# Seven block products for five pairs of w_down's row blocks, in a two-layer decoder on one core

## The chip, the cores and the metric

The kernel runs on one core of a Trainium2 chip. The metric is the device time of one execution in microseconds (us), lower is better. The chip's engines run side by side and wait for each other by semaphores: TensorE (PE; its weight loads are listed apart as PEld), VectorE (DVE), ScalarE (ACT), GpSimd (POOL), and SyncE (SP), which here issues the loads from HBM.

## The reference

Two decoder layers over 256 tokens of width 1024, in float32. Layer 0 has block-sparse attention (with 256 tokens, one causal block) and layer 1 a forgetting attention. What the change touches is the second half of each layer, the MLP with a hidden width of 4096:

```python
def squared_relu_mlp(x, w_up, w_down):
    return jnp.square(jax.nn.relu(x @ w_up)) @ w_down

# in each layer, h being 256 x 1024:
h = h + merge_heads(mix) @ w_o[layer]
h = h + squared_relu_mlp(rms_norm(h, mlp_norm[layer]), w_up[layer], w_down[layer])
# after the last layer
return rms_norm(h, final_norm)
```

w_down is 4096 x 1024 per layer, so the product with it has 256 rows, 4096 terms and 1024 columns.

## The kernel before, in words

Each float32 operand is split into a high part (`hi`, rounded) and the rest (`lo`), and a product is three matmuls: high by high, high by low and low by high. For a weight, `split` (L143) makes both parts: ACT copies a piece of 128 x 1024 values to `hi` (L148), and DVE subtracts to get `lo` (L149).

Weights come in chunks of 1 MB by one DMA each, into three buffers called `raw` (pool `wraw`). There are seven buffers for high parts and seven for low parts (`whi`, `wlo`), each for one piece of 128 x 1024; a chunk fills two. A list `plan` holds the order of all chunks. `chunk(i)` (L191) is called by every step that multiplies; it sees to it that the loads and splits up to two chunks further on have been written into the program. A load waits for its `raw` buffer, that is for the last DVE instruction on the chunk three places earlier. A split waits for the `hi` and `lo` buffers, that is for the last matmul on the piece seven places earlier.

A row block of w_down is 128 of its 4096 rows; there are 32. The hidden activations `hid` are kept transposed, as 32 blocks of 128 x 256 (two halves of 128 tokens), high and low. With `row_chunk` (L153) a chunk of w_down is four row blocks by 512 columns. `mm_rows` (L196) multiplies one half of one hidden block by one row block into a PSUM bank of 128 x 512: three matmuls of 512 columns. The product is run first for columns 0 to 511 (nb=0) over all 32 blocks and both halves, then for columns 512 to 1023 (nb=1): 2 x 32 x 2 x 3 = 384 matmuls per layer. After each nb, `down_done` (L780) adds the two banks to `h`. In layer 0 the norm of the next layer then begins on these columns (`norm_steps`, L279), while TensorE goes on with nb=1.

In layer 1 the code after the loop (L799 to L824) runs nb=1: all blocks but the last eight for both halves in turn, then the last eight for half 0, then for half 1, and after each half the final norm of that half: add to `h` (L778), sum of squares on ACT (L813), mean on DVE (L815), the power -0.5 on POOL (L818), the scaling on ACT and DVE (L820, L823), and two output DMAs.

Before the product with w_down, `put_up` (L713) makes the hidden blocks two at a time from PSUM: ACT copies one part (L723), DVE adds the other (L724), squares (L726), ACT rounds to the high part (L727) and DVE subtracts (L728). This is the up stage; a chunk of w_up holds two hidden blocks.

The order of TensorE is written out by a planner (`Weave`) that takes steps from lists by due times; within w_down the steps stand in the order in which the code makes them. The order of DVE and ACT is chosen by a scheduler when the program is built; each engine then runs its instructions strictly in that order.

PSUM has eight banks, in three pools: `psa` (three, tiles named acc), `pss` (four, sc), `psv` (one, pv). The small work tiles `t` (pool `tmp`) have six buffers.

Of the kernel before, what the change touches and what calls it, by code (L numbers as in the profile page):

```python
# [8 lines left out]
F32 = mybir.dt.float32  # L9
# [5 lines left out]
P = 128  # L15
D = 1024
# [46 lines left out]
def yoco_kernel(  # L63
# [160 lines left out]
    hid = []

# [382 lines left out]
    for layer in range(2):  # L608
# [99 lines left out]


        hid.clear()  # L710


        def put_up(fc, accs):  # L713
# [12 lines left out]
            nc.vector.scalar_tensor_tensor(sq[:, 0:n], u[:, 0:n], 0.0, u[:, 0:n], op0=ALU.max, op1=ALU.mult)  # L726
            nc.scalar.copy(hh[:, a], sq[:, 0:n])  # L727
# [52 lines left out]
        def down_done(nb, ps):  # L780
# [5 lines left out]
            if layer:  # L786

                nc.vector.tensor_scalar(part, sums[:, :, 0], 1.0 / D, EPS, op0=ALU.mult, op1=ALU.add)

        edge = []  # L790
        for nb in range(2 - layer):
            fill += rows_steps(take(FF // NB), hid, lambda ps, nb=nb: down_done(nb, ps),
                               pe.after((("h", nb, 0), 850), (("h", nb, 1), 1500)))
# [5 lines left out]
    cs = take(FF // NB)  # L799
    ps = [psa.tile([P, NB], F32, name="acc") for _ in range(2)]  # L800

    def last_part(half, k):
        mm_rows(ps[half], *hidden(k), half, chunk(cs[k // CK]), k % CK, k == 0, k == FF // P - 1)

    for k in range(FF // P - 2 * CK):
        for half in range(2):
            last_part(half, k)
    for half in range(2):
        for k in range(FF // P - 2 * CK, FF // P):
            last_part(half, k)  # L810
        add_mlp(1, half, ps[half])
# [42 lines left out]
```

## Time and profile before

| | us |
|---|---|
| median of three runs (lowest to highest) | 599.67 (599.61 to 599.84) |
| the profiled execution | 599.86 |
| its span, first to last instruction and DMA | 598.1 |
| TensorE busy in the span | 587.9 |
| VectorE busy | 399.2 |
| ScalarE busy | 325.2 |

The profiled execution is 1.76 us longer than its span. Busy shares are averages over stages. In the trace of before, the up stage of layer 0 lies at about 121 to 210 us, its w_down at 210 to 298 us; those of layer 1 lie at about 414 to 503.5 us and 503.5 to 590.8 us. A matmul's listed length (0.39 us) overlaps with its neighbours'; what it costs in a row of matmuls is the distance from start to start. The granted TensorE clock was 0.998 of full speed over the execution.

### The profile page before, as it was taken

What the parts mean: (1) busy time and instruction counts of PE and PEld (TensorE: products, weight loads), DVE (VectorE), ACT (ScalarE), POOL (GpSimd) and SP (SyncE); (2) the same over time, 40 slices, a digit from 0 to 9 for tenths busy, and PEclk for the clock granted to TensorE, in tenths of its full rate; (3) what the DMA queues carried; (4) which work ended last, traced back from release to release, by engine and by line L of the source; (5) the groups of instructions that cost most, each with busy time, mean ns of one, the idle gap of its engine ahead of it and who ended that gap; (6) DMA issues with size and microseconds to landing.
All of it is one profiled execution on the core that took longest, in us unless ns stands there. A gap on an engine that the chain in (4) does not pass through costs nothing.

```text
span 598.1 us, 8745 instructions
## 1 busy us (share of the span) xinstructions
PE 587.9 (98%) x3412; PEld 506.0 (85%) x3412; DVE 399.2 (67%) x715; ACT 325.2 (54%) x563; POOL 10.1 (2%) x39
## 2 busy tenths in 40 slices
PE   8999999999999999999999999999999999999995
PEld 6998997888888888888889989978888888888884
DVE  5887477488877854564588976668788778446422
ACT  6776566566655644363474664666666555334411
POOL 3000000000000000000000000000000000000000
PEclk9999999999999999999999999999999999999999
DMA  8974443467655655555546444543766656555401
GB/s 269 315 267 141 141 141 88 131 190 227 208 169 187 211 187 171 206 196 182 185 143 210 141 142 141 173 143 94 213 188 208 171 184 212 186 178 199 142 0 72
DMA packets 77034, 103.94 MB, mean 174 GB/s; under 512 B 1800, under 2 KB 51504, under 8 KB 76992
## 3 DMA queue, kind: packets, MB, share of 16 engines
q1 hardware_dynamic: 76480, 102.26, 52.8%
q8 instruction: 27, 0.44, 0.3%
q0 software_dynamic: 208, 0.59, 0.3%
q10 hardware_dynamic: 304, 0.53, 0.2%
q14 instruction: 15, 0.12, 0.1%
HBM read 102.32 MB, written 1.05 MB: 173 GB/s over the span
## 4 chain that ended last, share of the span: by engine, by line
PE 97%; DMA 1%; SPq 0%; DVE 0%; ACT 0%; POOLq 0%; issue 0%
PE acc L216 19%; PE acc L199 14%; PE acc L201 14%; PE acc L200 14%; PE acc L220 9%; PE acc L207 5%; PE acc L209 5%; PE acc L208 5%; PE sc L356 2%; PE pv L368 1%; DMA h<-in_x_dram 1%; PE sc L216 1%; PE sc L324 1%; PE sc L322 1%; PE sc L269 1%; PE sc L220 1%
## 5 line engine op out<-in xcount | busy, mean ns | idle before, releaser
L149 DVE TENSOR_TENSOR lo<-raw,hi 128x1024 fp32r<-128x1024 f32 x188 | 229.0, 1222 | 114.0 <-ACT hi L148 113.0
L148 ACT ACTIVATE hi<-raw 128x1024 fp32r<-128x1024 f32 x188 | 198.4, 1061 | 133.8 <-PE acc L201 99.4
L216 PE MATMUL acc<-x,hi 128*128 128x512 f32 x480 | 164.6, 396 | 0.0
L199 PE MATMUL acc<-hi,b 128*128 128x512 f32 x320 | 126.3, 395 | 0.0
L201 PE MATMUL acc<-hi,b 128*128 128x512 f32 x320 | 124.8, 390 | 0.0
L200 PE MATMUL acc<-lo,b 128*128 128x512 f32 x320 | 124.6, 390 | 0.0
L220 PE MATMUL acc<-x,lo 128*128 128x256 f32 x480 | 124.3, 279 | 0.0
L216 PEld LDWEIGHTS acc<-x,hi 128*128 128x128 f32 x480 | 86.1, 188 | 16.2
L220 PEld LDWEIGHTS acc<-x,lo 128*128 128x128 f32 x480 | 90.5, 189 | 5.3
L207 PE MATMUL acc<-x,hi 128*128 128x256 f32 x256 | 74.1, 289 | 0.0
L209 PE MATMUL acc<-x,lo 128*128 128x256 f32 x256 | 72.4, 283 | 0.0
L208 PE MATMUL acc<-x,hi 128*128 128x256 f32 x256 | 72.4, 283 | 0.0
L199 PEld LDWEIGHTS acc<-hi,b 128*128 128x128 f32 x320 | 60.1, 188 | 12.9 <-issue 1.0
L201 PEld LDWEIGHTS acc<-hi,b 128*128 128x128 f32 x320 | 60.1, 188 | 12.8
L200 PEld LDWEIGHTS acc<-lo,b 128*128 128x128 f32 x320 | 60.2, 188 | 11.9
L723 ACT COPY t<-acc 128x256 f32<-128x256 f32 x60 | 22.4, 373 | 63.6 <-PE acc L216 61.1
L207 PEld LDWEIGHTS acc<-x,hi 128*128 128x128 f32 x256 | 49.0, 191 | 1.8 <-issue 1.7
L208 PEld LDWEIGHTS acc<-x,hi 128*128 128x128 f32 x256 | 49.0, 192 | 0.1
L209 PEld LDWEIGHTS acc<-x,lo 128*128 128x128 f32 x256 | 49.0, 192 | 0.0
L724 DVE TENSOR_TENSOR t<-acc,t 128x256 f32<-128x256 f32 x60 | 25.0, 420 | 20.5 <-ACT t L723 20.4
L341 ACT ACTIVATE t<-t,nm 128x128 f32<-128x128 f32 x64 | 28.3, 443 | 7.6 <-DVE nm L334 7.6
L727 ACT CAST b<-t 128x512 fp32r<-128x512 f32 (+1 forms) x36 | 20.6, 571 | 6.7 <-DVE t L726 6.7
(129 smaller groups left out, 523.6 us busy)
## 6 DMA issues: line engine op xcount, KB each, us to landing
raw<-in_w_up_dram SPq DMA_DIRECT2D x32, 1024.0 KB, 5.5
raw<-in_w_down_dram SPq DMA_DIRECT2D x32, 1024.0 KB, 5.1
raw<-in_moba_w_qkv_dram SPq DMA_DIRECT2D x10, 1024.0 KB, 5.2
raw<-in_w_o_dram SPq DMA_DIRECT2D x8, 1024.0 KB, 4.9
raw<-in_w_kv_dram SPq DMA_DIRECT2D x8, 1024.0 KB, 5.4
raw<-in_fox_w_q_dram SPq DMA_DIRECT2D x4, 1024.0 KB, 4.9
raw<-in_moba_w_qkv_dram SPq DMA_DIRECT2D x3, 512.0 KB, 7.9
h<-in_x_dram SPq DMA_DIRECT2D x2, 256.0 KB
```

The source lines that it names most:

```text
L148: nc.scalar.activation(hi[:, i:i + n], raw[:, i:i + n], AF.Copy)
L149: nc.vector.tensor_sub(lo[:, i:i + n], raw[:, i:i + n], f(hi[:, i:i + n]))
L199: nc.tensor.matmul(ps, xh[:, kx, t], hi[:, kw % 2], start=start, stop=False)
L200: nc.tensor.matmul(ps, xh[:, kx, t], lo[:, kw % 2], start=False, stop=False)
L201: nc.tensor.matmul(ps, xl[:, kx, t], hi[:, kw % 2], start=False, stop=stop)
L207: nc.tensor.matmul(ps, hi[:, k], xh[:, k], start=k == 0, stop=False)
L208: nc.tensor.matmul(ps, hi[:, k], xl[:, k], start=False, stop=False)
L209: nc.tensor.matmul(ps, lo[:, k], xh[:, k], start=False, stop=k == KC - 1)
L216: nc.tensor.matmul(ps, hi[:, k], x2[:, k].rearrange("p t s -> p (t s)"), start=k == 0, stop=k == KC - 1)
L220: nc.tensor.matmul(ps[:, 0:S], lo[:, k], xh[:, k], start=False, stop=False)
L341: nc.scalar.activation(pes[hd][:, b], lg[:, b], AF.Exp, bias=nm[:, t:t + 1], scale=-1.0, accum_out=sums[:, t:t + 1])
L724: nc.vector.tensor_add(u[:, j], ps[:, 0:S], cp)
```

## The change

The list of w_down's work is new. The first 24 of the 32 row blocks form 12 pairs; a chunk is now one pair with all 1024 columns (`pair_chunk`). `MIXED` says for each pair whether it is multiplied whole ("W": seven pairs) or by seven block products ("S", Strassen's scheme in Winograd's form: pairs 2, 4, 6, 8 and 10). The last eight row blocks (`REST`) are multiplied as before, four blocks by 512 columns at a time.

A whole pair takes, for each of its two blocks, the four combinations of half and column half, three matmuls each: 24 matmuls. A seven pair regards hidden activations and weights as 2 x 2 block matrices (two blocks by two halves of tokens; two blocks by two column halves) and needs seven block products instead of eight: 21 matmuls. For this it forms four sums on each side:

- for the weights, on DVE (`seven_pair`): four additions or subtractions of 128 x 512, three splits instead of two (plain blocks, first sums, second sums), and a fourth sum, t1, that is split by a small copy on ACT and a subtraction on DVE;
- for the activations, in `put_up`: three small additions on DVE (128 x 256, 128 x 128, 128 x 128), and one more rounding and subtraction of 128 x 384; they are stored in a new tile `both_` of the pool `act`.

Sums that belong to one output block alone go into its bank directly (`acc`, four banks of `pss`); four products are collected over all five seven pairs in banks of their own (`prod`: w, u2, u3 in `psa`, u1 in `psv`) and are combined and added to `h` once per layer (`put_products`: one copy on ACT, four additions and four adds to `h` on DVE). So during w_down all eight banks are in use. Then comes `REST` for nb=0 with `down_done`, then for nb=1.

At the very end half 1 leaves out the last two row blocks (`LAST`), adds its bank to `h`, and then multiplies these two blocks in two pieces of 256 columns, each with a bank, an add to `h`, a sum of squares and a mean of its own (`add_last`, `square`, `mean`, `finish`).

```diff
+MIXED = [("W", 0), ("W", 1), ("S", 2), ("W", 3), ("S", 4), ("W", 5), ("S", 6), ("W", 7), ("S", 8), ("W", 9), ("S", 10), ("W", 11)]
+SEVEN = [p for kind, p in MIXED if kind == "S"]
+REST = range(2 * len(MIXED), FF // P)
...
+    def pair_chunk(w, p):
+        raw = wraw.tile([P, 2, D], F32, name="raw")
+        nc.sync.dma_start(raw, w[2 * p * P:(2 * p + 2) * P].rearrange("(c p) n -> p c n", p=P))
+        return raw
+
+    def whole_pair(w, p):
+        raw = pair_chunk(w, p)
+        return [split(raw[:, k].rearrange("p (n c) -> p n c", c=NB)) for k in range(2)]
+
+    def seven_pair(w, p):
+        raw = pair_chunk(w, p)
+        left, right = raw[:, :, 0:NB], raw[:, :, NB:D]
+        t1 = tmp.tile([P, 1, NB], F32, name="t")
+        nc.vector.tensor_add(t1, left[:, 0:1], right[:, 0:1])
+        nc.vector.tensor_add(right[:, 0], right[:, 0], right[:, 1])
+        plain = split(left)
+        th, tl = (tmp.tile([P, 1, NB], F32R, name="t") for _ in range(2))
+        nc.vector.tensor_add(left[:, 0], left[:, 0], right[:, 0])
+        nc.vector.tensor_add(left[:, 1], left[:, 1], left[:, 0])
+        sums = split(right)
+        nc.scalar.activation(th, t1, AF.Copy)
+        nc.vector.tensor_sub(tl, t1, f(th))
+        more = split(left)
...
-        plan += [(row_chunk, w_down[layer], k0, nb * NB) for nb in range(2) for k0 in range(0, FF // P, CK)]
+        plan += [({"W": whole_pair, "S": seven_pair}[kind], w_down[layer], p) for kind, p in MIXED]
+        plan += [(row_chunk, w_down[layer], k0, nb * NB) for nb in range(2) for k0 in REST[::CK]]
...
             nc.vector.scalar_tensor_tensor(sq[:, 0:n], u[:, 0:n], 0.0, u[:, 0:n], op0=ALU.max, op1=ALU.mult)
+            if fc // 2 in SEVEN:
+                us = tmp.tile([P, 3, P], F32, name="t")
+                a11, a12, a21 = sq[:, 0, 0:P], sq[:, 1, 0:P], sq[:, 0, P:S]
+                nc.vector.tensor_sub(us[:, 0:2], sq[:, 0].rearrange("p (t s) -> p t s", s=P), sq[:, :, P:S])
+                nc.vector.tensor_sub(us[:, 2], us[:, 1], a11)
+                nc.vector.tensor_add(a21, us[:, 2], a12)
...
+            if fc // 2 in SEVEN:
+                nc.scalar.copy(diffs[0][:, at], us)
+                nc.vector.tensor_sub(diffs[1][:, at], us, f(diffs[0][:, at]))
...
+        def seven_part(c, p, i):
+            n = SEVEN.index(p)
+            place, at, factor = (
+                (prod["w"], hidden_part(2 * p, 0), "b11"), (acc[0, 0], hidden_part(2 * p + 1, 0), "b21"),
+                (acc[0, 1], hidden_part(2 * p, 1), "b22"), (prod["u3"], 0, "t3"), (prod["u1"], 1, "t1"),
+                (prod["u2"], 2, "t2"), (acc[1, 0], hidden_part(2 * p + 1, 1), "t4"))[i]
...
+    for k in range(FF // P - 2 * CK, FF // P - LAST):
+        last_part(1, k, FF // P - LAST)
+    add_last(1, ps[1], 0, NB)
+    sums_of = part[:, 1:2]
+    for n0, (pool, name) in ((0, (psa, "acc")), (S, (psa, "acc"))):
+        p = pool.tile([P, S], F32, name=name)
+        for k in range(FF // P - LAST, FF // P):
...
+                nc.tensor.matmul(p, st[:, kx, t], mv[:, k % 2, n0:n0 + S], start=k == FF // P - LAST and mv is hi and st is xh,
+                                 stop=k == FF // P - 1 and st is xl)
+        add_last(1, p, n0, n0 + S)
+        sums_of = mean(square(1, n0, n0 + S), sums_of)
+    finish(1, sums_of)
```

How the instructions stand on the engines. The rows below are the built program's; line numbers of the changed program are its own: L260 to L262 are the three matmuls of a block product in a pair (`mm_parts`), L154 is the subtraction that makes `lo` (L149 of before), L184, L185, L188 and L189 are the four sums of weights in `seven_pair` in the order of the code, L192 makes the low part of t1. The number in a `raw` name tells the chunks apart: in layer 0 raw_2436 is pair 3 (whole), raw_2470 pair 4 (seven), raw_2514 pair 5 (whole), raw_2548 pair 6 (seven).

TensorE in the middle of w_down of layer 0, before: one piece (hi_2240, lo_2241, two row blocks), the two halves in turn into two banks.

```order
L199 MATMUL acc_2350<-hi_2240,b0_1500 128x512
L200 MATMUL acc_2350<-lo_2241,b0_1500 128x512
L201 MATMUL acc_2350<-hi_2240,b2_1502 128x512
L199 MATMUL acc_2351<-hi_2240,b0_1500 128x512
L200 MATMUL acc_2351<-lo_2241,b0_1500 128x512
L201 MATMUL acc_2351<-hi_2240,b2_1502 128x512
```

The same place in the changed program: the third to fifth of the seven block products of pair 4 (b is a hidden block, x2_1438 the new tile `both_`, pv_2388 the bank of u1, t_2479 and t_2480 the parts of t1).

```order
L260 MATMUL sc_2383<-hi_2483,b0_1501 128x512
L261 MATMUL sc_2383<-lo_2484,b0_1501 128x512
L262 MATMUL sc_2383<-hi_2483,b2_1503 128x512
L260 MATMUL acc_2387<-hi_2483,x2_1438 128x512
L261 MATMUL acc_2387<-lo_2484,x2_1438 128x512
L262 MATMUL acc_2387<-hi_2483,x2_1438 128x512
L260 MATMUL pv_2388<-t_2479,x2_1438 128x512
L261 MATMUL pv_2388<-t_2480,x2_1438 128x512
L262 MATMUL pv_2388<-t_2479,x2_1438 128x512
```

Every block product is still three matmuls of 512 columns; what differs is the bank and the operand, and that a pair has 21 of them or 24.

DVE in w_down of layer 0, before: one subtraction after the other, two for each chunk.

```order
L149 TENSOR_TENSOR lo_2393<-raw_2386,hi_2392 128x1024
L149 TENSOR_TENSOR lo_2423<-raw_2420,hi_2422 128x1024
L149 TENSOR_TENSOR lo_2427<-raw_2420,hi_2426 128x1024
L149 TENSOR_TENSOR lo_2457<-raw_2454,hi_2456 128x1024
L149 TENSOR_TENSOR lo_2461<-raw_2454,hi_2460 128x1024
```

The same stage in the changed program, from the last piece of pair 3 to the second of pair 5.

```order
L154 TENSOR_TENSOR lo_2443<-raw_2436,hi_2442 128x1024
L154 TENSOR_TENSOR lo_2476<-raw_2470,hi_2475 128x1024
L154 TENSOR_TENSOR lo_2484<-raw_2470,hi_2483 128x1024
L188 TENSOR_TENSOR raw_2470<-raw_2470 128x512
L189 TENSOR_TENSOR raw_2470<-raw_2470 128x512
L184 TENSOR_TENSOR t_2550<-raw_2548 128x512
L154 TENSOR_TENSOR lo_2490<-raw_2470,hi_2489 128x1024
L185 TENSOR_TENSOR raw_2548<-raw_2548 128x512
L154 TENSOR_TENSOR lo_2517<-raw_2514,hi_2516 128x1024
L154 TENSOR_TENSOR lo_2521<-raw_2514,hi_2520 128x1024
```

The sum L184 on pair 6 now stands in front of the last piece of pair 4 and of both pieces of pair 5. Pair 6 is loaded into the buffer of pair 3, which the first row of this fence sets free.

DVE at the very end of layer 1, before: the two halves' adds, means and scalings.

```order
L778 SCALAR_TENSOR_TENSOR h_88<-acc_5444,r2_4375,h_88 128x512
L815 SCALAR_TENSOR_TENSOR ms_5677<-sums_5157,part_5160 128x1
L823 SCALAR_TENSOR_TENSOR x2_5158<-h_88,r_5679,x2_5158 128x512
L778 SCALAR_TENSOR_TENSOR h_88<-acc_5445,r2_4375,h_88 128x512
L815 SCALAR_TENSOR_TENSOR ms_5712<-sums_5157,part_5160 128x1
L823 SCALAR_TENSOR_TENSOR x2_5158<-h_88,r_5714,x2_5158 128x512
```

The same in the changed program, for half 1 alone.

```order
L927 SCALAR_TENSOR_TENSOR h_88<-sc_5292,r2_4473,h_88 128x512
L927 SCALAR_TENSOR_TENSOR h_88<-acc_5899,r2_4473,h_88 128x256
L927 SCALAR_TENSOR_TENSOR h_88<-acc_5912,r2_4473,h_88 128x256
L937 SCALAR_TENSOR_TENSOR ms_5910<-sq_5908,part_5288 128x1
L937 SCALAR_TENSOR_TENSOR ms_5923<-sq_5921,ms_5910 128x1
L946 SCALAR_TENSOR_TENSOR x2_5286<-h_88,r_5925,x2_5286 128x512
```

Half 1 has three adds in place of one, the last two of 256 columns, and both means stand behind the last add.

## Rows read from the trace of the kernel before

**Rows 1.** The page: busy time of each engine with its share of the span and number of instructions, and the chain of work that ended last, by engine.

```profile
PE 587.9 (98%) x3412; PEld 506.0 (85%) x3412; DVE 399.2 (67%) x715; ACT 325.2 (54%) x563; POOL 10.1 (2%) x39
...
PE 97%; DMA 1%; SPq 0%; DVE 0%; ACT 0%; POOLq 0%; issue 0%
```

**Rows 2.** Busy time by stretch. Columns: stretch, its length, busy time (instructions) of PE, PEld, DVE, ACT and POOL, granted clock, mean busy share of the DMA engines, GB/s. The stretches are the up stage of layer 0, the two halves of w_down in layer 0, the up stage of layer 1, and w_down in layer 1.

```profile
127.00:204.00 77.00, 77.00 (x443) 67.11 (x442) 62.63 (x90) 47.10 (x74) 0.00 (x0) 1.00 0.61 193
210.00:256.00 46.00, 46.00 (x206) 38.03 (x205) 23.69 (x23) 19.98 (x23) 0.00 (x0) 1.00 0.56 189
256.00:300.00 44.00, 44.00 (x200) 36.54 (x199) 23.53 (x27) 20.60 (x29) 0.00 (x0) 1.00 0.56 188
421.00:498.00 77.00, 77.00 (x442) 67.10 (x441) 63.14 (x90) 47.10 (x74) 0.00 (x0) 1.00 0.63 192
503.50:548.00 44.50, 44.50 (x198) 36.83 (x197) 22.37 (x22) 18.56 (x19) 0.00 (x0) 1.00 0.55 190
```

**Rows 3.** TensorE in order of time in w_down of layer 1: start, length, line, output and input. Twelve matmuls of 512 columns lie from the first row's start to the last row's.

```profile
541.67 0.39 PE L199 MATMUL acc<-hi,b 128*128 128x512 f32 x1
541.90 0.39 PE L200 MATMUL acc<-lo,b 128*128 128x512 f32 x1
542.12 0.39 PE L201 MATMUL acc<-hi,b 128*128 128x512 f32 x1
...
544.39 0.39 PE L199 MATMUL acc<-hi,b 128*128 128x512 f32 x1
```

**Rows 4.** The same view early in layer 0, with matmuls of 256 columns; twelve lie from the first row's start to the last row's.

```profile
21.00 0.28 PE L209 MATMUL acc<-x,lo 128*128 128x256 f32 x1
...
22.44 0.28 PE L209 MATMUL acc<-x,lo 128*128 128x256 f32 x1
```

**Rows 5.** Groups of instructions with their shapes kept apart: line, engine, operation, output and input, shapes, count; busy us and mean ns of one; idle time before them and what ended it.

```profile
L149 DVE TENSOR_TENSOR lo<-raw,hi 128x1024 fp32r<-128x1024 f32 x188 | 229.0, 1222 | 114.0 <-ACT hi L148 113.0
L148 ACT ACTIVATE hi<-raw 128x1024 fp32r<-128x1024 f32 x188 | 198.4, 1061 | 133.8 <-PE acc L201 99.4 <-PE acc L208 28.5 <-DMA raw<-in_moba_w_qkv_dram 3.1
...
L724 DVE TENSOR_TENSOR t<-acc,t 128x256 f32<-128x256 f32 x60 | 25.0, 420 | 20.5 <-ACT t L723 20.4
...
L728 DVE TENSOR_TENSOR b<-t,b 128x512 fp32r<-128x512 f32 x28 | 19.2, 684 | 0.0
...
L727 ACT CAST b<-t 128x512 fp32r<-128x512 f32 x28 | 17.4, 621 | 6.7 <-DVE t L726 6.7
...
L778 DVE SCALAR_TENSOR_TENSOR h<-acc,r,h 128x512 f32<-128x512 f32 x8 | 5.7, 744 | 13.5 <-PE acc L201 13.5
...
L407 DVE TENSOR_TENSOR wfx<-wf,wfx 128x128 fp32r<-128x128 f32 x1 | 0.3, 283 | 0.0
```

**Rows 6.** DVE in order of time in the up stage of layer 0: start, length, line. Neighbours without a bracket at the end waited for nothing.

```profile
144.14 0.69 DVE L726 SCALAR_TENSOR_TENSOR t<-t 128x512 f32<-128x512 f32 x1
144.75 1.22 DVE L149 TENSOR_TENSOR lo<-raw,hi 128x1024 fp32r<-128x1024 f32 x1
145.89 0.69 DVE L728 TENSOR_TENSOR b<-t,b 128x512 fp32r<-128x512 f32 x1
146.49 0.42 DVE L724 TENSOR_TENSOR t<-acc,t 128x256 f32<-128x256 f32 x1
```

**Rows 7.** Loads. First the range over the loads that L155 issues (w_down among them); then two loads of w_up that followed each other, their issue (start of the first, time to the end of the second, count), and the time from issue to landing of each; then one load early in the run, when several were under way.

```profile
DMA to landing us min/median/max: 4.9/5.1/7.6
...
102.19 3.15 SPq L161 DMA_DIRECT2D raw<-in_w_up_dram  x2
...
raw<-in_w_up_dram SPq DMA_DIRECT2D x1, 1024.0 KB, 5.6
...
raw<-in_w_up_dram SPq DMA_DIRECT2D x1, 1024.0 KB, 6.8
...
raw<-in_moba_w_qkv_dram SPq DMA_DIRECT2D x1, 1024.0 KB, 8.5
```

**Rows 8.** The change from the up stage to w_down in layer 0, in order of time: the first matmul of w_down, and the first addition of DVE on the last bank of the up stage.

```profile
210.14 0.40 PE L199 MATMUL acc<-hi,b 128*128 128x512 f32 x1
...
210.80 0.42 DVE L724 TENSOR_TENSOR t<-acc,t 128x256 f32<-128x256 f32 x1 [0.69 <-ACT t L723]
```

**Rows 9.** The end of the run in order of time: the last matmul and what follows it.

```profile
590.44 0.39 PE L201 MATMUL acc<-hi,b 128*128 128x512 f32 x1
590.86 0.75 DVE L778 SCALAR_TENSOR_TENSOR h<-acc,r,h 128x512 f32<-128x512 f32 x1 [2.26 <-PE acc L201]
591.65 0.63 ACT L813 ACTIVATE t<-h 128x512 f32<-128x512 f32 x1 [3.07 <-DVE h L778]
592.18 0.19 ACT L813 ACTIVATION_READ_ACCUMULATOR t<-h 128x1 f32 x1
592.40 0.16 DVE L815 SCALAR_TENSOR_TENSOR ms<-sums,part 128x1 f32<-128x1 f32 x1 [0.79 <-ACT t L813]
592.71 0.55 POOL L818 TENSOR_TENSOR r<-ms,mhalf 128x1 f32<-128x1 f32 x1 [4.88 <-DVE ms L815]
593.29 0.75 DVE L823 SCALAR_TENSOR_TENSOR x<-h,r,x 128x512 f32<-128x512 f32 x1 [0.73 <-POOL r L818]
594.08 0.35 ACTq L824 DMA_DIRECT2D out_dram<-x  x1
```

More of the change, by code (lines that the diff above doesn't have):

```diff
@@ L222, in mm_apart, with mm_parts @@
             both()
+    def mm_parts(ps, x, w, start, stop):
+        nc.tensor.matmul(ps, x[0], w[0], start=start, stop=False)
+        nc.tensor.matmul(ps, x[0], w[1], start=False, stop=False)
+        nc.tensor.matmul(ps, x[1], w[0], start=False, stop=stop)
     hid = []
@@ L788, in down_done @@
                 nc.vector.tensor_scalar(part, sums[:, :, 0], 1.0 / D, EPS, op0=ALU.mult, op1=ALU.add)
-        edge = []
-        for nb in range(2 - layer):
-            fill += rows_steps(take(FF // NB), hid, lambda ps, nb=nb: down_done(nb, ps),
-                               pe.after((("h", nb, 0), 850), (("h", nb, 1), 1500)))
+        acc = {(half, nb): pss.tile([P, NB], F32, name="sc") for nb in range(2) for half in range(2)}
+        prod = {name: psa.tile([P, NB], F32, name="acc") for name in ("w", "u2", "u3")}
@@ new lines, in put_products, with add @@
+        def put_products():
+            def add(half, nb, t):
+                hs = h[:, half, nb * NB:(nb + 1) * NB]
+                nc.vector.scalar_tensor_tensor(hs, t, r2[:, half:half + 1], hs, op0=ALU.mult, op1=ALU.add)
+            first, q_, z = (tmp.tile([P, NB], F32, name="t") for _ in range(3))
+            nc.scalar.copy(first, prod["w"])
+            nc.vector.tensor_add(q_, prod["u2"], first)
+            nc.vector.tensor_add(z, prod["u3"], q_)
+            add(0, 0, prod["w"])
+            add(1, 0, z)
+            nc.vector.tensor_sub(q_, prod["u1"], q_)
+            nc.vector.tensor_sub(z, prod["u1"], z)
+            add(0, 1, q_)
+            add(1, 1, z)
@@ new lines, in yoco_kernel, with rest_part @@
+        edge = []
+        for i, (kind, p) in zip(take(len(MIXED)), MIXED):
+            if kind == "W":
+                fill += [((), 1300, lambda i=i, p=p, j=j: whole_part(chunk(i), p, j), None) for j in range(2)]
+            else:
+                fill += [((), 650, lambda i=i, p=p, n=n: seven_part(chunk(i), p, n), None) for n in range(7)]
+        fill.append(((), 0, put_products, None))
+        for nb in range(2 - layer):
+            cs = take(len(REST) // CK)
+            def rest_part(nb, cs, k, half):
+                mm_rows(acc[half, nb], *hidden(k), half, chunk(cs[(k - REST[0]) // CK]), k % CK, False, k == REST[-1])
+                if (k, half) == (REST[-1], 1):
+                    down_done(nb, [acc[t, nb] for t in range(2)])
+            fill += [((), 648, lambda nb=nb, cs=cs, k=k, half=half: rest_part(nb, cs, k, half),
+                      pe.after((("h", nb, 0), 850), (("h", nb, 1), 1500)) if (k, half) == (REST[-1], 1) else None)
+                     for k in REST for half in range(2)]
@@ L796, in yoco_kernel @@
                 edge += norm_steps(nb, [(gs[:, 2], *xkv[:2]), (gs[:, 1], *xa[:2])])
[L799 to L811, printed above, removed]
+    cs = take(len(REST) // CK)
@@ L812, in yoco_kernel, with last_chunk, last_part, add_last @@
+    ps = [acc[half, 1] for half in range(2)]
+    def last_chunk(k):
+        return chunk(cs[(k - REST[0]) // CK])
+    def last_part(half, k, n):
+        mm_rows(ps[half], *hidden(k), half, last_chunk(k), k % CK, False, k == n - 1)
+    LAST = 2
+    def add_last(half, psum, n0, n1):
+        hs = h[:, half, NB + n0:NB + n1]
+        nc.vector.scalar_tensor_tensor(hs, psum, r2[:, half:half + 1], hs, op0=ALU.mult, op1=ALU.add)
+    def square(half, n0, n1):
         junk = tmp.tile([P, NB], F32, name="t")
-        nc.scalar.activation(junk, h[:, half, NB:D], AF.Square, accum_out=sums[:, half, 1:2])
+        sq = small.tile([P, 1], F32, name="sq")
+        nc.scalar.activation(junk[:, n0:n1], h[:, half, NB + n0:NB + n1], AF.Square, accum_out=sq)
+        return sq
@@ L814, in yoco_kernel, with mean, finish @@
+    def mean(sq, before):
         ms = small.tile([P, 1], F32, name="ms")
-        nc.vector.scalar_tensor_tensor(ms, sums[:, half, 1:2], 1.0 / D, part[:, half:half + 1],
-                                       op0=ALU.mult, op1=ALU.add)
+        nc.vector.scalar_tensor_tensor(ms, sq, 1.0 / D, before, op0=ALU.mult, op1=ALU.add)
+        return ms
+    def finish(half, ms):
         rf = small.tile([P, 1], F32, name="r")
         nc.gpsimd.tensor_tensor(rf, ms, mhalf[:, 0:1], op=ALU.pow)
-        hg = ys[:, half, 0:NB]
```

40 lines of the change are left out of this document (35 added, 5 removed).

## The prediction

> **What bounds the kernel now.** I read the page first: TensorE is busy for 98% of the span and makes up 97% of the chain that ended last, VectorE (DVE) is busy for 67% [rows 1]. Averages hide stages, so the table of stretches comes next. TensorE is full in every stretch that the change touches, while DVE is at 62.63 of 77 us (81%) in the up stage of layer 0, 63.14 of 77 in that of layer 1, and at about half (23.69 of 46, 23.53 of 44, 22.37 of 44.5) in w_down [rows 2]. So a matmul removed is time removed, as long as DVE, which must pay for it with additions, stays ahead of TensorE. In w_down the splitting engines run ahead now: ACT's 133.8 us of idle time before its high parts ended mostly with a matmul that set a weight buffer free, 3.1 us with a DMA [rows 5]. The weights wait for TensorE, not the other way round.
>
> **TensorE.** Twelve matmuls of 512 columns go from 541.67 to 544.39, so one costs 2.72/12 = 0.2267 us [rows 3]; twelve of 256 columns take 1.44 us, 0.120 each [rows 4]. A seven pair has 21 matmuls in place of 24. Five pairs in each of two layers: 30 matmuls fewer, 30 x 0.2267 = 6.80 us. The last two blocks of half 1 become 12 matmuls of 256 columns in place of 6 of 512: 1.44 - 1.36 = +0.08 us. Everything else on TensorE only changes banks and operands.
>
> The Trainium skill (TensorE: Matmul & The Clock Gate, "Back-to-back issue gap") gives N/2.4 + 2.5 ns for warm matmuls in a row, an estimate of 0.2158 us for 512 columns and 0.109 for 256. By it the saving would be 6.47 us and the split of the end nearly free; the rows of this kernel show 5 to 10% more per matmul, and I keep the rows.
>
> **The end.** After the last matmul (590.44) come an add of 0.75, a square of 0.63 with its read 0.19, a mean of 0.16, the power 0.55, the scaling 0.75 and the DMA [rows 9]. The last add and the last square now have 256 columns. A DVE add of 256 takes 0.42 against 0.744 for this one [rows 5]: -0.32. For the square I take the same share off its 0.63, about -0.25. The second mean is 0.16 more on DVE, but the first fits while ACT squares the second piece, since in the new order both adds stand in front of both means. Together about -0.5. Bounds: -0.6 if all of it counts, +0.5 if the two pieces line up one behind the other.
>
> **The up stage.** Five chunks of each layer get three small DVE sums and a subtraction. 256 columns 0.42, 128 columns 0.283 twice, and 384 columns between the rows for 256 and 512 (0.42 and 0.684), 0.55: 1.53 us [rows 5]. A chunk of w_up is two subtractions of 1.222, two adds of 0.42 and two operations of about 0.69: 4.67 us of DVE beside 16 pairs of matmuls (0.2267 + 0.120), 5.55 us. With the addition it is 6.2, 0.65 too long, but these chunks alternate with plain ones that have 0.88 to spare. For the stage: 62.63 + 7.65 = 70.3 of 77 us, 91% [rows 2]. I cost it at nothing: the cover is the two chunks of split weights and the third PSUM bank. If that cover failed, each of the five chunks would cost 0.65, 3.3 us a layer, 6.5 in all. It cannot gain.
>
> **DVE in w_down.** Per seven pair: five operations of 128 x 512 (four sums, the low part of t1) at 0.684 and three subtractions at 1.222, together 7.1 us [rows 5], beside 21 x 0.2267 = 4.76 us of TensorE. A whole pair: 2.44 beside 5.44. From pair 2 to pair 10 they alternate, and one of each makes 9.53 us of DVE for 10.20 of TensorE, 93%. ACT has five pieces of 1.061 and a copy of 0.621, 5.9 us: no bound. So DVE keeps up on average, and what counts is the order and the buffers.
>
> The first test is the lead at the start. DVE takes up the last bank of the up stage 0.66 us after w_down begins (210.14 to 210.80) [rows 8]. Until the first piece of pair 3 its new order then has one operation of 256 columns, ten of 512 and three subtractions of 1.222: 0.66 + 0.42 + 6.84 + 3.67 = 11.6 us. TensorE wants that piece after two whole pairs and a seven, 69 matmuls or 15.64 us. Lead 4.0; I say 3.5, for hand-overs.
>
> The second is a loop that before did not have. Pair 6 can be loaded only when pair 3 has left its `raw` buffer, and in DVE's order the first sum on pair 6 stands in front of the last piece of pair 4 and both of pair 5. From one whole pair freed to the next: landing L, then 0.684 + 1.222 + 0.684 + 2 x 1.222 = 5.03, with hand-overs about 5.2. The loop is L + 5.2 against TensorE's 10.20, and it is run three times (pair 3 to 5, 7, 9). TensorE then waits 3 x (L - 5.0) - 3.5 us per layer, if that is above nothing. A lone load of this kind lands in 5.1 us (4.9 to 7.6) [rows 7]: no wait. But the buffer of a seven pair is set free about 3 us before that of a whole pair, so two loads overlap. In w_up, two that were issued 2.8 us apart (3.15 - 0.37) landed in 5.6 and 6.8, 1.2 more for the second [rows 7]. So I take L = 5.1 + 1.2 = 6.3: 0.4 us per layer.
>
> Against that stands that neighbours on DVE overlap: a subtraction listed with 1.22 is followed after 1.14, an operation of 0.69 after 0.60 [rows 6]. With 0.08 off each of five instructions the loop is 0.4 shorter and the wait is nothing. The Trainium skill (VectorE: DVE Perf Modes, "The DRAIN you can't avoid") says that the next operation does not start until the pipeline is empty; by that nothing overlaps, both layers lose 0.4 and the sum would end 0.6 higher. The rows do show starts before the listed end of the one before, so I lean to the overlap and take 0.1 per layer. Bounds per layer: nothing at L = 5.1; 4.3 at 7.6; 7.0 at the 8.5 that a load took early in the run [rows 7]. It cannot gain.
>
> **Smaller parts.** `put_products` is once per layer four adds of 0.744 and four of 0.684 on DVE, 5.7 us, beside the 27 us of TensorE that follow pair 10 and hold only 12 us of subtractions: nothing. If it were uncovered it would be 5.7 a layer, but `h` is wanted only at `down_done`, 16 us after pair 10. In layer 0 the norm of nb=0 has 10.9 us of nb=1 beside it now (48 matmuls) in place of 43.5: enough for its few us, and the order of the next layer's steps is as it was. All eight banks are taken during w_down; the next user of each waits for an add that it needed anyway.
>
> **The sum**, against the profiled execution's 599.86: -6.80 + 0.08 - 0.50 + 0.2 = 592.8. The median of the runs shown is 599.67, 0.2 lower, well inside what I can claim.
>
> **Rivals.**
> 1. The raw loop makes TensorE wait in earnest, but less than is saved. For it: 93% of DVE, and a first sum that waits for a load in front of work that is ready. Against it: the lead of 3.5 us and the overlap. At L = 6.8 it is 1.9 per layer, 3.8 in all: 596.4.
> 2. The up stage. For it: chunks of 6.2 us of DVE beside 5.55. Against it: plain chunks between. Price up to 6.5: 592.6 + 6.5 = 599.1, no change; half of it 595.9.
> 3. Slower: the same loop with loads that land late for every whole pair. From L = 7.4 on (3 x 2.4 - 3.5 = 3.7 per layer) it eats all that is saved; at 8.5 it is 14 us in all, 606.6. For it: 8.5 was seen when several loads were under way, and 7.6 once through L155. Against it: the load per us of TensorE is nearly what it was, and the DMA engines were at 0.55 to 0.56 there [rows 2].
> 4. The change doesn't save what it says, because products with the new operands run at another rate. Against it: same shapes, same weight loads. I give it nothing of its own.
>
> **How the numbers follow.** The forecast, 592.0 to 594.0: 0.66. Rival 1, 594 to 598.5: 0.20. Rival 2: 0.05, a fifth of it no change. Rival 3, slower: 0.05. The remaining 0.04 is a somewhat larger gain at the end, below 592. A measurement of this kernel can tell about 0.2%, 1.2 us, from no change. Faster by more than that, below 598.5: 0.66 + 0.19 + 0.04 + 0.04 = 0.93, rounded to 0.92; within: 0.03; slower: 0.05. The range that leaves out 2 in 10 begins at 592.0 and ends in rival 1, at 597.0; the forecast's own range is 592.0 to 594.0.
>
> **What the profile of the changed kernel would show.** 24 matmuls fewer; 21 matmuls from the start of a seven pair to its end in 4.76 us; DVE at about 90% from pair 2 to pair 10, with short waits of L184 for a DMA and none of TensorE for DVE; about 0.5 us less from the last matmul to the first mean's power. Wrong would be: gaps on TensorE at the last piece of pair 6 or 8 or at the first of pair 9 (rival 1 or 3, and the landing times tell which), gaps in the up stage (rival 2), or a pair of 21 matmuls that takes longer than 4.8 us without a wait.

## The result and the profile after

The changed kernel takes 592.46 us (median; 591.63 to 592.50 in 4 runs) against 599.64 (599.47 to 599.84) for the kernel before beside it: ratio 0.9877, 95% interval 0.986 to 0.9894. The forecast was 592.8. The profiled execution has a span of 590.8 us, 7.3 less than before.

The page of the changed kernel, busy time and chain, answers to [rows 1]:

```profile
PE 581.8 (98%) x3388; PEld 501.0 (85%) x3388; DVE 462.7 (78%) x834; ACT 341.8 (58%) x597; POOL 10.1 (2%) x39
...
PE 97%; DMA 1%; SPq 0%; DVE 0%; ACT 0%; issue 0%; POOLq 0%; DVEq 0%; ACTq 0%
```

There are 24 matmuls fewer (30 fewer in the pairs, 6 more from the divided end). VectorE does 63.5 us more work, and TensorE still makes up 97% of the chain. Busy time by stretch, the columns as in [rows 2]: the up stage of layer 0, w_down of layer 0 with the pairs and then behind them, and the pairs of layer 1.

```profile
127.00:204.00 77.00, 77.00 (x442) 67.08 (x442) 69.06 (x110) 48.08 (x79) 0.00 (x0) 1.00 0.64 193
210.00:272.00 62.00, 62.00 (x276) 51.30 (x275) 54.32 (x63) 34.22 (x38) 0.00 (x0) 1.00 0.55 197
272.00:294.00 22.00, 22.00 (x103) 18.31 (x102) 16.31 (x22) 12.56 (x20) 0.00 (x0) 1.00 0.56 181
503.00:565.00 62.00, 62.00 (x275) 51.34 (x275) 55.81 (x64) 34.18 (x38) 0.00 (x0) 1.00 0.54 192
```

TensorE is full in every stretch. DVE is at 90% in the up stage (69.06 of 77) and at 88 and 90% beside the pairs (54.32 and 55.81 of 62). In the whole execution TensorE waits only for the start-up, as the view of waits shows (engine, line, what it waited for; total us, times, longest):

```profile
PE sc L586 <- DVE ones L110: 1.1, 1, 1.1
PE sc L555 <- DMA h<-in_x_dram: 1.0, 1, 1.0
```

DVE meets the load of the next seven pair as forecast. Its rows in order of time (five pieces from the last of pair 2 to the second of pair 4, the first sum on pair 6, the last piece of pair 4, then three pieces of which the first is pair 5's), under them the first matmul of pair 5, and what the view of line L172 (the loads of pairs) says of landing times:

```profile
219.09 5.77 DVE L154 TENSOR_TENSOR lo<-raw,hi 128x1024 fp32r<-128x1024 f32 x5 [0.53 <-ACT hi L153]
...
228.03 0.69 DVE L184 TENSOR_TENSOR t<-raw 128x512 f32<-128x512 f32 x1 [1.85 <-DMA raw<-in_w_down_dram]
228.64 1.22 DVE L154 TENSOR_TENSOR lo<-raw,hi 128x1024 fp32r<-128x1024 f32 x1
...
230.38 3.49 DVE L154 TENSOR_TENSOR lo<-raw,hi 128x1024 fp32r<-128x1024 f32 x3
```

```profile
235.93 0.39 PE L260 MATMUL sc<-hi,b 128*128 128x512 f32 x1
```

```profile
DMA to landing us min/median/max: 4.6/4.8/5.8
```

DVE stands still for 1.85 us in front of pair 6, and TensorE does not notice: pair 5's first piece ends at 231.60, 4.3 us before TensorE begins that pair. The loads land in 4.6 to 5.8 us. On TensorE a seven pair takes what 21 matmuls take, as the start of its first block product and that of the next pair's first show:

```profile
220.97 0.39 PE L260 MATMUL acc<-hi,b 128*128 128x512 f32 x1
...
225.73 0.39 PE L260 MATMUL sc<-hi,b 128*128 128x512 f32 x1
```

225.73 - 220.97 = 4.76 us. The end, which answers to [rows 9]: the last matmul, the two squares (L932) with the read of the first, the two means (L937), and the issue of the last output.

```profile
583.70 0.28 PE L967 MATMUL acc<-hi,b 128*128 128x256 f32 x1
584.03 0.42 ACT L932 ACTIVATE t<-h 128x256 f32<-128x256 f32 x1 [2.34 <-DVE h L927]
584.35 0.19 ACT L932 ACTIVATION_READ_ACCUMULATOR t<-h 128x1 f32 x1
584.54 0.42 ACT L932 ACTIVATE t<-h 128x256 f32<-128x256 f32 x1
584.57 0.16 DVE L937 SCALAR_TENSOR_TENSOR ms<-sq,part 128x1 f32<-128x1 f32 x1
...
585.08 0.16 DVE L937 SCALAR_TENSOR_TENSOR ms<-sq,ms 128x1 f32<-128x1 f32 x1 [0.35 <-ACT t L932]
...
586.76 0.35 ACTq L947 DMA_DIRECT2D out_dram<-x  x1
```

The last matmul starts at 583.70 instead of 590.44, 6.74 earlier. From it to the output's issue it is 3.06 us instead of 3.64, 0.58 less. Together 7.32, all of the span's difference.

### The profile page after: what moved, and what is told of

Same layout as the page of the kernel before. It is cut to its first block, busy times and chain, and to the rows that moved or that the text cites. A ratio compares the mean times of both kernels' runs of the same rounds, so it can differ in the third digit from the quotient of the medians.

```text
span 590.8 us, 8877 instructions
## 1 busy us (share of the span) xinstructions
PE 581.8 (98%) x3388; PEld 501.0 (85%) x3388; DVE 462.7 (78%) x834; ACT 341.8 (58%) x597; POOL 10.1 (2%) x39
## 4 chain that ended last, share of the span: by engine, by line
PE 97%; DMA 1%; SPq 0%; DVE 0%; ACT 0%; issue 0%; POOLq 0%; DVEq 0%; ACTq 0%
PE acc L250 19%; PE acc L254 9%; PE sc L260 5%; PE sc L261 5%; PE sc L262 5%; PE acc L241 5%; PE acc L242 5%; PE acc L243 5%; PE acc L233 5%; PE acc L235 4%; PE acc L234 4%; PE sc L234 2%; PE sc L235 2%; PE sc L233 2%; PE sc L396 2%; PE pv L408 1%
## 5 line engine op out<-in xcount | busy, mean ns | idle before, releaser
L154 DVE TENSOR_TENSOR lo<-raw,hi 128x1024 fp32r<-128x1024 f32 x198 | 238.5, 1220 | 46.4 <-ACT hi L153 45.3
L153 ACT ACTIVATE hi<-raw 128x1024 fp32r<-128x1024 f32 x198 | 205.8, 1058 | 111.2 <-DVE raw L189 35.7
L260 PE MATMUL sc<-hi,b 128*128 128x512 f32 x142 | 55.3, 389 | 0.0
L262 PE MATMUL sc<-hi,b 128*128 128x512 f32 x142 | 55.2, 389 | 0.0
L261 PE MATMUL sc<-lo,b 128*128 128x512 f32 x142 | 55.2, 389 | 0.0
L262 PEld LDWEIGHTS sc<-hi,b 128*128 128x128 f32 x142 | 26.6, 188 | 5.6
L261 PEld LDWEIGHTS sc<-lo,b 128*128 128x128 f32 x142 | 26.7, 188 | 5.5
L260 PEld LDWEIGHTS sc<-hi,b 128*128 128x128 f32 x142 | 26.7, 188 | 5.5
L233 PE MATMUL acc<-hi,b 128*128 128x512 f32 x64 | 26.6, 415 | 0.0
```

The costliest lines, as they stand in the source:

```text
L153: nc.scalar.activation(hi[:, i:i + n], raw[:, i:i + n], AF.Copy)
L154: nc.vector.tensor_sub(lo[:, i:i + n], raw[:, i:i + n], f(hi[:, i:i + n]))
L233: nc.tensor.matmul(ps, xh[:, kx, t], hi[:, kw % 2], start=start, stop=False)
L260: nc.tensor.matmul(ps, x[0], w[0], start=start, stop=False)
L261: nc.tensor.matmul(ps, x[0], w[1], start=False, stop=False)
L262: nc.tensor.matmul(ps, x[1], w[0], start=False, stop=stop)
```

## The experiments

What the experiments try: whether the matmuls left out and the divided end pay by themselves, and whether DVE's 63.5 us more stay hidden because seven pairs alternate with whole ones, loads land in about 5 us, and enough of w_down is left behind the last pair. The rivals: the saving lies in the rearrangement; DVE has room anywhere and the order does not matter; the loop through the load buffer would hurt. Line numbers of the experiments' kernels differ by a few from those of the changed kernel. The runs lie on several chips; each ratio is to the kernel before, timed on the same chip.

**All pairs whole.**

```diff
-MIXED = [("W", 0), ("W", 1), ("S", 2), ("W", 3), ("S", 4), ...
+MIXED = [(k, p) for p, k in enumerate("WWWWWWWWWWWW")]
...
```

The edit also leaves out what only seven pairs use: the tile `both_`, the four banks `prod` and `put_products`.

> All twelve pairs are multiplied whole, 24 matmuls each; chunks of whole pairs, banks and the divided end stay as in the changed kernel. Theory (the matmuls left out pay, the rest of the rearrangement is worth only the 0.5 us of the end): 30 matmuls of 0.2267 us come back, 592.5 + 6.8 = 299.2 + 300 = 599.3 us, between 599.0 and 599.6. Rival (the new chunks and banks themselves save part): clearly below, 596 or less. Rival (seven pairs cost hidden TensorE waits that whole pairs don't): also below 599.

Measured: 599.35 us (598.91 to 599.51), ratio 0.9985 (0.9975 to 0.9995). The first matmul of w_down in layer 0 and the last matmul of the run, first of this kernel and then the first one of the changed kernel:

```profile
209.68 0.40 PE L260 MATMUL sc<-hi,b 128*128 128x512 f32 x1
...
590.11 0.28 PE L967 MATMUL acc<-hi,b 128*128 128x256 f32 x1
```

```profile
210.07 0.40 PE L260 MATMUL sc<-hi,b 128*128 128x512 f32 x1
```

590.11 - 209.68 = 380.43 us here, 583.70 - 210.07 = 373.63 in the changed kernel: 6.80 apart, 30 times 0.2267. The new chunks, and the four banks that they are summed in, save nothing by themselves.

**The end not divided.**

```diff
-    for k in range(FF // P - 2 * CK, FF // P - LAST):
-        last_part(1, k, FF // P - LAST)
+    for k in range(FF // P - 2 * CK, FF // P):
+        last_part(1, k, FF // P)
     add_last(1, ps[1], 0, NB)
...
-    finish(1, sums_of)
+    finish(1, mean(square(1, 0, NB), part[:, 1:2]))
```

> The seven pairs stay; the end of half 1 is as before: its last eight blocks in 512 columns, one add, one square, one mean. Theory: the way from the last matmul to the output grows by the 0.58 us that the two traces differ in there, and two blocks in 512 columns take 0.08 us less on TensorE: 592.5 + 0.5 = 593.0 us. Rival (the end is as long either way, the gain is all matmuls): 592.4. The profile's end decides: from the last matmul's start to the issue of the last output 3.6 us (theory) or 3.1 us (rival).

Measured: 592.93 us (592.75 to 593.13). The end of this kernel in order of time:

```profile
583.59 0.39 PE L235 MATMUL sc<-hi,b 128*128 128x512 f32 x1
584.01 0.75 DVE L927 SCALAR_TENSOR_TENSOR h<-sc,r,h 128x512 f32<-128x512 f32 x1 [2.23 <-PE sc L235]
...
587.29 0.35 ACTq L947 DMA_DIRECT2D out_dram<-x  x1
```

From the last matmul to the output's issue it is 3.70 us against 3.06, near the theory's 3.6. The medians differ by 0.47 us, but the two kernels were timed beside different runs of the kernel before (medians 599.96 and 599.64), and their ratios to it are both 0.9877. So the trace shows this step, and the times alone do not.

**The seven pairs next to each other.**

```diff
-MIXED = [("W", 0), ("W", 1), ("S", 2), ("W", 3), ("S", 4), ...
+MIXED = [(k, p) for p, k in enumerate("WWSSSSSWWWWW")]
```

> The same five seven pairs, one behind the other (pairs 2 to 6), then whole pairs: as many matmuls as the changed kernel. Theory (the mixing with whole pairs is what keeps VectorE ahead): a seven pair takes 6.4 us (with overlap) to 7.1 us of VectorE beside 4.76 of TensorE; from the first piece of pair 3 on four of them lose 6.6 to 9.4 us, against a lead of 4 to 4.5: TensorE waits 2 to 5.5 us per layer for the parts of a weight, 4 to 11 in all, 597 to 603 us, likeliest 600. Rival (VectorE's lead or buffers take it, order doesn't matter): 592.5, no waits of TensorE.

Measured: 603.23 us (602.89 to 603.62), ratio 1.0051 (1.0031 to 1.0071): slower than the kernel before, with the same 3388 matmuls as the changed kernel, and just above the 597 to 603 expected. TensorE in w_down of layer 0, the matmuls that waited:

```profile
235.50 0.50 PE L261 MATMUL acc<-lo,x 128*128 128x512 f32 x1 [1.50 <-DVE lo L154]
240.85 0.50 PE L260 MATMUL acc<-hi,x 128*128 128x512 f32 x1 [0.52 <-ACT hi L153]
242.12 0.50 PE L261 MATMUL acc<-lo,x 128*128 128x512 f32 x1 [0.76 <-DVE lo L154]
...
248.64 0.50 PE L261 MATMUL acc<-lo,x 128*128 128x512 f32 x1 [0.77 <-DVE lo L154]
```

The wait comes in the third seven pair, when the lead is used up, and then in each: 242.12 to 248.64 is 6.52 us for a pair of 4.76. That is VectorE's time with overlap (6.4 forecast), together with ACT, whose high part now also comes late. Each layer loses about 5.2 us. The alternation is what hides DVE's work. Side result: here five chunks of w_up with the additional sums follow each other, and the up stage loses nothing (w_down begins at 209.80).

**Six seven pairs, among fourteen and among twelve.**

```diff
-MIXED = [("W", 0), ("W", 1), ("S", 2), ("W", 3), ("S", 4), ...
+MIXED = [(k, p) for p, k in enumerate("WWSWSWSWSWSWSW")]
...
+    extra = const.tile([P, 2, 3, P], F32R, name="extra")
```

The new tile holds the sums of the sixth pair; to make room, a small constant tile (`nd`) shares a buffer with later work. With four row blocks left at the end of layer 1, half 1 has two blocks in 512 columns behind the end of half 0, not six.

> Fourteen pairs with six seven pairs, four row blocks left for the end of w_down. Theory (TensorE is still the only bound, VectorE at about 90% beside it): 6 matmuls fewer, 6 x 0.2267 = 1.36 us: 591.1 us. Rival (the lead of VectorE is used up, or the combined products, which now have 12 us less of TensorE beside them, come late): 592.5 or more, with waits of TensorE behind the last pairs or at the first columns' end.

Measured: 593.21 us (592.93 to 593.51): no gain, a miss. Two matmuls that waited in this kernel, and the end of its run:

```profile
296.40 0.98 PE L309 MATMUL sc<-ident,h 128*128 128x128 f32 x7 [0.23 <-DVE h L835]
...
323.18 0.71 PE L495 MATMUL sc<-parts,sel 128*128 128x256 f32 x4 [1.00 <-DVE parts L479]
...
583.87 0.28 PE L967 MATMUL acc<-hi,b 128*128 128x256 f32 x1
...
584.61 0.71 ACT L947 ACTIVATE x<-x,r 128x512 f32<-128x512 f32 x1
585.22 0.40 ACT L935 ACTIVATE t<-h 128x256 f32<-128x256 f32 x1
...
587.43 0.35 ACTq L950 DMA_DIRECT2D out_dram<-x  x1
```

DVE and ACT come out of w_down late. The next norm's transposes (L309) wait for the add to `h` (0.4 us longer from start to start than between their neighbours), the decays of layer 1 (L495) for a chain of small DVE operations, and at the very end the scaling of half 0 stands on ACT in front of the last square, so that the end takes 3.56 us instead of 3.06. With four blocks behind the last pair, the work that was costed at nothing is in the way. The next run puts the sixth pair among twelve, with eight blocks behind:

```diff
-MIXED = [(k, p) for p, k in enumerate("WWSWSWSWSWSWSW")]
+MIXED = [(k, p) for p, k in enumerate("WWSWSWSWSWSS")]
```

> Six seven pairs among twelve pairs (2, 4, 6, 8, 10 and 11), eight row blocks left behind them as in the changed kernel; two seven pairs are neighbours at the end. In the run with six among fourteen pairs the matmuls saved 1.2 us and the work of VectorE behind w_down (four row blocks instead of eight beside the combined products) gave back 0.4 at the next norm, 1.0 at the decays of layer 1 and 0.5 at the very end. Theory (what failed there was the cover behind the last pair): with eight blocks behind it the 6 x 0.2267 = 1.36 us stay, less the two neighbours, which take 6.5 us of VectorE beside 4.76 but find a lead of 4 us: 591.1 us. Rival (a sixth seven pair uses up VectorE's room anywhere): 592.5 or more, with waits of TensorE at pair 11 or behind it.

Measured: 591.57 us (591.17 to 593.48). This range reaches beyond the changed kernel's, so the two were timed beside each other.

> The changed kernel itself beside the next run, so that the two stand on one chip: 592.5 us.

> The kernel with six seven pairs among twelve pairs once more, beside the changed kernel. Theory (6 matmuls of 0.2267 us less, and nothing given back): 1.0 to 1.4 us below the changed kernel on the same chip, 591.1 to 591.5. Rival (the 0.9 us seen before is the spread from run to run): no difference above 0.3.

Measured: 592.20 us (592.11 to 592.43) for the changed kernel, ratio 0.9875 (0.986 to 0.9889); 591.33 (591.06 to 591.76) for six in twelve, ratio 0.9861 (0.9844 to 0.9877). The ranges of the two do not overlap, though the intervals of their ratios to the kernel before do: 0.9 us less, a little under the 1.0 to 1.4 expected, and the fastest of the kernels here. DVE behind the pairs in this kernel:

```profile
272.00:294.00 22.00, 22.00 (x103) 18.30 (x102) 20.10 (x27) 13.18 (x21) 0.00 (x0) 1.00 0.70 232
```

TensorE waits for nothing in w_down here, and DVE has 1.9 us left of the 22 behind the pairs: little is left there for a seventh pair of this kind, which was not tried. Between its first matmul of w_down in layer 0 and its last of the run lie 372.47 us, 1.16 less than in the changed kernel, where 1.36 was expected; the 0.2 was not followed.

**A late load.** The prediction's slower rival rests on the load of a seven pair.

```diff
+        if p in SEVEN:
+            nc.sync.dma_start(raw[:, 0:1], w[2 * p * P:(2 * p + 1) * P].rearrange("(c p) n -> p c n", p=P))
         nc.sync.dma_start(raw, w[2 * p * P:(2 * p + 2) * P].rearrange("(c p) n -> p c n", p=P))
```

> Each seven pair's weights are loaded with half of them (512 KB) sent ahead and then overwritten by the whole load, so that they land later: about 8 to 8.5 us after the buffer is free instead of 4.6 to 5.8. Theory (the loop from one freed buffer to the next is landing time + 5.2 us less 0.4 of overlap, against 10.20 us of TensorE, and is run three times a layer, with a lead of 4 to 4.5 us before it): 3 x (8.25 - 5.4) - 4.3 = 4.2 us of TensorE waits a layer, 8.5 in all: about 601 us, 598 to 603, slower than before the change. TensorE then waits for the parts of pairs 6, 8 and 9, VectorE for the load at its first sum. Rival (the load is hidden whatever it takes, as before the change): 592.5.

Measured: 592.43 us (591.96 to 592.72): a miss. DVE in order of time around the first sums (L186 here) on pair 6 and pair 8 and the pieces of pair 9, and under them the first matmuls of pairs 7 and 9:

```profile
227.69 3.50 DVE L154 TENSOR_TENSOR lo<-raw,hi 128x1024 fp32r<-128x1024 f32 x3 [1.19 <-ACT hi L153]
232.03 0.69 DVE L186 TENSOR_TENSOR t<-raw 128x512 f32<-128x512 f32 x1 [0.84 <-DMA raw<-in_w_down_dram]
...
242.13 0.69 DVE L186 TENSOR_TENSOR t<-raw 128x512 f32<-128x512 f32 x1 [1.69 <-DMA raw<-in_w_down_dram]
242.74 2.36 DVE L154 TENSOR_TENSOR lo<-raw,hi 128x1024 fp32r<-128x1024 f32 x2
...
254.26 2.35 DVE L154 TENSOR_TENSOR lo<-raw,hi 128x1024 fp32r<-128x1024 f32 x2
```

```profile
246.45 0.39 PE L262 MATMUL sc<-hi,b 128*128 128x512 f32 x1
...
256.65 0.39 PE L262 MATMUL sc<-hi,b 128*128 128x512 f32 x1
```

The first load of pair 6 was issued at 222.93, and its sum ran at 232.03, 9.1 us later. But the three subtractions before it are the last piece of pair 4 and both of pair 5, which in the changed kernel stand behind the sum. That the scheduler moved the sum back because it knew of the double load when the program was built is inferred; the rows show only the new order. So the first round of the loop was not in this program.

The other two rounds were. The sums on pairs 8 and 10 (242.13 and 253.66) stand in front of both pieces of pairs 7 and 9, and came 10.9 and 8.6 us after the last subtraction on pairs 5 and 7 (231.19 and 245.10) had set the buffer free. In layer 0 the first piece of pair 5 was ready 6.2 us before TensorE began that pair, the first piece of pair 7 only 2.5 us before, that of pair 9 only 1.2 (in layer 1: 6.2, 3.6 and 2.8). The late load did cost VectorE up to 5 us of its lead, and the lead, longer here because pair 5's pieces had gone ahead, just covered it. To try the loop in all its rounds, the order has to be held.

**The order held, with the load in time and late.** In `split`, for the pieces of pairs 5, 7 and 9; `after` is a column of the next pair's weights, whose load is now written ahead of these pieces:

```diff
+        if after is not None:
+            nc.vector.tensor_copy(lo[:, 0, 0:1], after)
```

For the second of the two kernels, besides:

```diff
+        for _ in range(2 if p in SEVEN[2:] else 1):
+            nc.sync.dma_start(raw, w[2 * p * P:(2 * p + 2) * P].rearrange("(c p) n -> p c n", p=P))
```

> In the run with the late load no time was lost, but VectorE's order had changed there: both pieces of pair 5 stood in front of the first sum on pair 6. Here two copies of one column (128 x 1) from the loaded pair 6, 8 or 10 into the low parts of pair 5, 7 or 9 hold the pieces of the whole pair behind that load, and nothing is loaded twice. Theory (with landings of 4.6 to 5.8 us the order is harmless): 592.5 us, within 0.3, no waits of TensorE in w_down. Rival (the order itself costs): 594 or more.

> The same, and pairs 6, 8 and 10 are loaded twice in full, one load behind the other, so that they are there about 9.6 to 10.3 us after their buffer is free. Theory (where VectorE must pass the late load before the pieces of the whole pair, the loop from one whole pair freed to the next sets the pace): landing + 0.2 + 0.6 + 2 x 1.14 = landing + 3.1, so 12.7 to 13.4 us against 10.20 of TensorE. The first round is covered (pair 5's first piece 0.9 to 1.6 us ahead of TensorE), the second and third are late by 1.0 to 2.5 and 2.5 to 3.3: 3.6 to 5.8 us a layer, 7 to 12 in all: 600 to 604 us, no longer faster than before the change. TensorE waits for the parts of pairs 7 and 9. Rival (a late load is hidden in any order): 592.5.

Measured: 592.64 us (591.72 to 592.82) with the load in time, where TensorE waits for nothing in w_down: the order alone is harmless. 604.27 (603.65 to 605.78) with the load late, ratio 1.0079 (1.0063 to 1.0096). In the late kernel DVE's copies that wait for pairs 6, 8 and 10 in layer 0, with the two subtractions on pair 5:

```profile
232.48 0.21 DVE L153 CAST lo<-raw 128x1 fp32r<-128x1 f32 x2 [4.00 <-DMA raw<-in_w_down_dram]
...
233.21 2.35 DVE L156 TENSOR_TENSOR lo<-raw,hi 128x1024 fp32r<-128x1024 f32 x2
...
245.54 0.21 DVE L153 CAST lo<-raw 128x1 fp32r<-128x1 f32 x2 [2.74 <-DMA raw<-in_w_down_dram]
...
258.36 0.22 DVE L153 CAST lo<-raw 128x1 fp32r<-128x1 f32 x2 [2.50 <-DMA raw<-in_w_down_dram]
```

The rounds take 13.06 and 12.82 us. The second subtraction on pair 5 ends at 235.56 (two in a row of 2.35 from 233.21), 9.98 before the copy on pair 8: with a landing of 10.0 the loop is landing + 3.1, as worked out, against 10.20 of TensorE. What TensorE does with it in the third round, in order of time:

```profile
257.69 0.39 PE L271 MATMUL sc<-hi,b 128*128 128x512 f32 x1
260.36 0.50 PE L272 MATMUL sc<-lo,b 128*128 128x512 f32 x1 [2.29 <-DVE lo L156]
...
261.18 0.53 PE L272 MATMUL sc<-lo,b 128*128 128x512 f32 x1
261.51 0.63 PE L273 MATMUL sc<-hi,b 128*128 128x512 f32 x1
261.93 0.63 PE L271 MATMUL sc<-hi,b 128*128 128x512 f32 x1
...
264.82 0.40 PE L272 MATMUL sc<-lo,b 128*128 128x512 f32 x1
```

In layer 0 the gap in the second round is 1.3 us long and in the third 2.4 (257.69 to 260.36 less one matmul), and in layer 1 they are 1.7 and 2.5 us. The rest of the loss lies behind the gap, in matmuls 0.43 apart; that is taken up in the last section. So a sum that waits for a late load in front of the whole pair's pieces makes this kernel slower than the one before.

## Why the prediction was right

**TensorE, -6.80 + 0.08.** The last matmul starts 6.74 us earlier, where -6.72 was forecast, and the kernel with whole pairs gives 6.80 between two matmuls of the trace. By the formula N/2.4 + 2.5 ns that the Trainium skill (TensorE: Matmul & The Clock Gate, "Back-to-back issue gap") gives, it would have been 6.47, an estimate. The same section calls this the gap of an isolated matmul, and puts a stream of weight loads and matmuls at about 131 ns for 512 columns, by which the saving would be 3.9 us, an estimate too; the prediction left that figure out. The trace agrees with neither, and the row's 0.2267 holds.

**The end, -0.5.** 0.58 in the trace. The step was right in what it said of the mean: the first (584.57) stands beside the second square (584.54). It slightly undersized the gain. The second square starts as the read of the first one ends (584.54); the second add ended at 584.51, so which of the two it waited for is not shown.

**The up stage, nothing.** DVE has 69.06 us of 77 where 70.3 was forecast, and no wait of TensorE. Even five such chunks in a row cost nothing there, so rival 2 had less for it than the prediction gave it.

**DVE in w_down.** The forecast of 93% of DVE from pair 2 to pair 10 stands beside 88 and 90% measured over the slightly longer stretch from pair 0 on. The lead at the start, taken as 3.5 us, was 4.3: pair 3's first piece (the second of the five subtractions from 219.09, 1.14 apart) ends at 221.45, and TensorE begins the pair at 225.73. It stays about that (4.3 at pair 5, 4.5 at pair 9), as it should where DVE has 9.5 us of work for every 10.20 of TensorE. With five seven pairs next to each other it is used up in the third.

**The loop, +0.2.** This is the term that was mis-sized, by little: L was taken as 6.3 because of two loads of w_up 2.8 us apart [rows 7], and these loads land in 4.6 to 5.8. So there was no wait to pay. That neighbours on DVE overlap is in the rows again: L184 of 0.69 at 228.03 is followed at 228.64, 0.08 before its listed end. The sentence of the Trainium skill that the prediction cites (VectorE: DVE Perf Modes, "The DRAIN you can't avoid") would let nothing start there before the end; the rows of before and after both show it starting. The same paragraph goes on that an operation that is not held starts earlier, and the section that it points to ("Two Vector instructions with no wait between them") makes only a held instruction wait for the ones before; with that the rows agree. The price of rival 3 was right in kind: with the order held and the load at 10.0, the loop lost 1.3 and 2.4 us in its second and third rounds and more behind them. Its condition was not met here. The number itself is not tried: the prediction's loop is landing + 5.2, with the last piece of the seven pair behind the sum, while in the late kernel that piece stands ahead of the copies and the loop is landing + 3.1. DVE's order as built, for which the price was worked out, was not run with a late load.

**`put_products`, nothing.** Right with eight blocks behind the last pair. With four, the adds and norms behind it cost 1.9 us (0.4, 1.0 and 0.5), so the cover that the prediction named, the work behind pair 10, was the one that counted.

The sum was 592.8 and the kernel is 0.3 below it: 0.2 of that is the loop, 0.1 the end, both by the trace.

## What to carry to other kernels

When the bound engine is full in a stretch, a matmul less is worth its distance from start to start, and the question is only whether the engine that pays keeps its lead. Work this out for each stretch from three things: the work per step on both engines, the lead at the first step, and the loops through buffers. Mix expensive steps with cheap ones, and leave work behind the last expensive one. An experiment on a program whose order a scheduler makes must hold that order, or it tries only part of what was meant.

## What was not expected of the hardware

TensorE's granted clock fell after a long gap, and a wait then cost more than its length. In the kernel with the order held and the load late, stretches of layer 0 in order of time, the columns as in [rows 2] (the granted clock stands behind POOL's 0.00):

```profile
257.00:260.00 3.00, 1.08 (x5) 0.56 (x3) 1.64 (x4) 1.58 (x2) 0.00 (x0) 1.00 1.03 422
261.00:264.50 3.50, 3.50 (x11) 2.67 (x10) 3.50 (x5) 1.06 (x1) 0.00 (x0) 0.54 0.55 152
265.00:272.00 7.00, 7.00 (x31) 5.46 (x31) 4.12 (x5) 3.74 (x5) 0.00 (x0) 1.00 0.12 46
```

TensorE had stood still for 2.4 us; 0.8 us after it took up work again the clock went to 0.54, about the level of 1.2 GHz, and came back about 3.3 us later. From 261.18 to 264.82 it is nine matmuls from start to start, 3.64 us, which at 0.2267 would take 2.04: 1.6 us on top of the wait. In layer 1 it was the same after a gap of 2.5 us: ten matmuls from 557.87 to 561.75, 3.88 us in place of 2.27, again 1.6 on top. Gaps of up to 1.7 us, in this kernel and in the one with neighbouring seven pairs, left the clock at 1.00 there; why it fell after the longer ones is not shown. The four gaps (1.3, 2.4, 1.7 and 2.5 us) and twice 1.6 make 11.1 of the 11.6 us between the two kernels with the order held. The forecast of 600 to 604 us did not have the term of the clock, and the result lay just above it; without its 3.2 us the kernel would be at about 601, still slower than before the change.
